# The five GpSimd sums of a pair for the second MLP product, put one at a time over the steps of the next pair

## The chip, the cores and the metric

The kernel runs on one NeuronCore of a Trainium2 chip. The engines have short names in the profile: PE is TensorE (matmuls), PEld its weight loads, DVE is VectorE, ACT is ScalarE, POOL is GpSimd, SP is the sync engine, whose queue issues the DMAs. Each engine works through its own queue in order, and waits for the others through semaphores. The metric is the device time of one execution in microseconds (us). Before the change it is 2529.06 us, the median of three runs (2527.83 to 2530.4).

## What is computed

Two layers of a decoder on 1024 tokens of width 1024. Each layer is an attention (the first a sparse one with compressed, selected and windowed keys, the second a sliding window with sinks) and an MLP, with norms and a conditioning vector `c` around both:

```python
def squared_relu_mlp(h, w_up, w_down):
    a = jax.nn.relu(h @ w_up)
    return (a * a) @ w_down

def reference(x, c, positions, ada_w, ada_b, norm_g, ...):
    cond = jax.nn.silu(c)
    for i in range(DEPTH):                       # 2
        mod = cond @ ada_w[i] + ada_b[i]
        sh1, sc1, g1, sh2, sc2, g2 = jnp.split(mod, 6, axis=-1)
        h = modulate(rms_norm(x, norm_g[i, 0]), sh1, sc1)
        ...                                      # attention gives y
        x = x + (1 + g1)[:, None, :] * rms_norm(y, norm_g[i, 1])
        h = modulate(rms_norm(x, norm_g[i, 2]), sh2, sc2)
        y = squared_relu_mlp(h, mlp_w_up[i], mlp_w_down[i])
        x = x + (1 + g2)[:, None, :] * rms_norm(y, norm_g[i, 3])
    return x
```

The change touches the MLP alone: `w_up` is 1024 x 4096, `w_down` is 4096 x 1024, all in f32.

## The kernel before

**Products.** Both MLP products are done with seven block products in place of eight, in the manner of Strassen and Winograd: sums and differences of blocks are formed first. Each f32 factor is split in a high part (a copy in a shorter format, `hi`) and the rest (`lo`), and three matmuls, hi times hi, lo times hi and hi times lo, stand for one (`mm3`, L572 to L574). A product of the first stage is twelve matmuls of 128x512.

**The up stage** (`mlp_up`) walks over 16 pairs `q` of column blocks of `w_up`. A pair needs seven products, in the order p = 1, 2, 6, 5, 7, 3, 4. For the first six pairs (`PAIRS0`) the products 1 and 2 are made ahead of all others, a stretch that the code calls the ramp. For each product a step of `prep` makes the weights, `AHEAD` products ahead:

```python
            elif p == 6:
                t(new(1), w[21], w[22], op=ALU.add)          # L1325, DVE
                t(new(2), sums[1], w[11], op=ALU.subtract)   # L1326, DVE
...
            elif p == 7:
                nc.gpsimd.tensor_tensor(r, w.pop(11), w.pop(21), op=ALU.subtract)   # L1332, POOL
...
            nc.scalar.activation(hi, r, AF.Copy)                                    # L1342, ACT
            nc.vector.tensor_tensor(lo, r, hi.bitcast(F32), op=ALU.subtract)        # L1343, DVE
```

L1336 is the like of L1332 for p = 3. So the weights of a product go DMA (`w`, L547), a sum on DVE or POOL (`ws`), the copy on ACT (`wt`), the rest on DVE (the same `wt`), PE. After a product, `evac` adds the PSUM bank `b` into the pair's tiles `u` (DVE, L1373), and ACT applies Relu (L1385) and Square (L1386), or copies (L1375).

**The five sums.** When a pair's last product is done, its four blocks of hidden values lie in two tiles `a` and `b` (both `u` in the trace). The second MLP product needs five sums or differences of these, which `combine` makes on POOL: four into two tiles `sx` (L1418), one into `sy` (L1429). SP writes them and two blocks of `u` to DRAM (`s`, L1422 to L1430), from where the down stage reads them. `combine` returns a list of stages; `chain` runs one stage and puts the next behind the following step.

**The order.** The Python steps are not the order on the engines. A scheduler takes the program order as priority, works out when operands will be ready, and lays out every engine's queue; then tiles get their buffers. Forty slots of 128x1024 f32 serve `sx`, `u`, `wt`, most raw weights `w`, and the tiles of the down stage together; a tile that takes a slot waits for the last reader of the one that had it. Conditioning weights (`adaw`, L311, multiplied on DVE by L321 and L323 into `ada`) are loaded and used in the gaps of the up stage. The first halves of `w` of later pairs and the `adaw` tiles share a ring of three buffers.

**The down stage** (`mlp_down`) then loads `w_down` (`wr`), sums it on POOL (L1476, L1477), splits it (`st`, ACT L1491 and DVE L1492) and multiplies.

Of the kernel before, what the change touches and what calls it, by code (L numbers as in the profile page):

```python
# [82 lines left out]
def spread(a, b):  # L83

    out, n = [], 0
    for k, f in enumerate(b):
        while n < len(a) and n * len(b) <= k * len(a):
            out.append(a[n])
            n += 1
        out.append(f)  # L90
    return out + a[n:]


class Trunk:
# [1271 lines left out]
    def mlp_up(self, up, side, sd, begin):  # L1366
        nc = self.nc
        R, order, before, left, _ = up
        U, banks, last = {}, {}, len(order) - 1

        def evac(q, p, o):
            a, b = U[q][0], U[q][-1]
            act, add = nc.scalar.activation, lambda out, y: nc.vector.tensor_tensor(out, o, y, op=ALU.add)  # L1373
            if p == 1:
                act(a[:, 1], o, AF.Copy)  # L1375
            elif p == 6:
                add(b[:, 0], a[:, 1])
            elif p == 5:
                add(a[:, 1], b[:, 0])
            else:  # L1380
                v, y = {2: (a[:, 0], a[:, 1]), 7: (b[:, 1], a[:, 1]), 3: (a[:, 1], a[:, 1]), 4: (b[:, 0], b[:, 0])}[p]
                add(v, y)
                if p == 7:
                    add(b[:, 0], b[:, 0])
                act(v, v, AF.Relu)  # L1385
                act(v, v, AF.Square)  # L1386

        def product(i):
            q, p = order[i]

            def part(j):
                if j == 0:
                    if p == 1:
                        U[q] = [self.slot("u", F32, [P, 2, 512])]
                    elif p == 6:
                        U[q].append(self.slot("u", F32, [P, 2, 512]))
                    banks[i] = self.bank()
                hi, lo = R[p][j]
                for z in range(2):
                    k = 2 * j + z  # L1400
                    s = tuple(left[i][:, y, k * P:(k + 1) * P] for y in range(2))
                    self.mm3(banks[i], s, (hi[:, z], lo[:, z]), k == 0, k == 3)
                if q == len(sd) - 1:
                    R[p][j] = None
                if j == 1:
                    left.pop(i)
                    evac(q, p, banks.pop(i))
            return [lambda j=j: part(j) for j in range(2)]

        def combine(q):  # L1410
            a, b = U.pop(q)
            d, z = sd[q], {}

            def two(n, *ops):
                def f():
                    z[n] = self.slot("sx", F32, [P, 2, 512])
                    for k, (x, y, op) in enumerate(ops):
                        nc.gpsimd.tensor_tensor(z[n][:, k], x, y, op=op)  # L1418
                return f

            def put():
                nc.sync.dma_start(d[:, 0], b[:, 1])  # L1422
                nc.sync.dma_start(d[:, 5], a[:, 0])
                nc.sync.dma_start(d[:, 1:3], z[0])

            def put2():
                nc.sync.dma_start(d[:, 3:5], z[1])
                v = self.t2("sy")
                nc.gpsimd.tensor_tensor(v, a[:, 1], b[:, 1], op=ALU.add)  # L1429
                nc.sync.dma_start(d[:, 6], v)  # L1430

            A, B = ALU.add, ALU.subtract
            return [two(0, (a[:, 0], b[:, 1], A), (b[:, 0], b[:, 1], B)), put,
                    two(1, (a[:, 0], b[:, 0], A), (a[:, 1], a[:, 0], B)), put2]

        ramp, steps = [], []
        for i, (q, p) in enumerate(order):
            own = spread(before(i), product(i))
            if p == 4:
                own.append(lambda q=q: self.later(lambda: self.chain(combine(q)), 1))  # L1440
            (ramp if i < 2 * PAIRS0 + 10 else steps).extend(own)
        self.go(ramp)
        self.go(spread(side, steps[:-LEAD_DOWN]) + spread(begin, steps[-LEAD_DOWN:]))
# [405 lines left out]
```

## Time and profile before

| | us |
|---|---|
| median of three runs | 2529.06 |
| lowest and highest | 2527.83, 2530.4 |
| the profiled execution | 2529.18 |
| its span in the trace | 2527.4 |
| PE busy in it | 2390.7 |
| DVE busy | 1924.7 |
| ACT busy | 1403.4 |
| POOL busy | 1323.6 |

The up stage of the first layer (layer 0) lies at about 950 to 1230 us of the trace and that of the second (layer 1) at about 1940 to 2220 us. Matmuls are pipelined: a matmul row shows 0.39 us, but in an unbroken stretch the next one starts about 0.22 us later. In the timelines, a number in brackets is how long the engine was idle ahead of the instruction, with what ended the wait.

### The profile page before, as it was taken

What the parts mean: (1) busy time and instruction counts of PE and PEld (TensorE: products, weight loads), DVE (VectorE), ACT (ScalarE), POOL (GpSimd) and SP (SyncE); (2) the same over time, 40 slices, a digit from 0 to 9 for tenths busy, and PEclk for the clock granted to TensorE, in tenths of its full rate; (3) what the DMA queues carried; (4) which work ended last, traced back from release to release, by engine and by line L of the source; (5) the groups of instructions that cost most, each with busy time, mean ns of one, the idle gap of its engine ahead of it and who ended that gap; (6) DMA issues with size and microseconds to landing.
All of it is one profiled execution on the core that took longest, in us unless ns stands there. A gap on an engine that the chain in (4) does not pass through costs nothing.

```text
span 2527.4 us, 36711 instructions
## 1 busy us (share of the span) xinstructions
PE 2390.7 (95%) x11974; PEld 1988.7 (79%) x11974; DVE 1924.7 (76%) x3723; ACT 1403.4 (56%) x2959; POOL 1323.6 (52%) x1308
## 2 busy tenths in 40 slices
PE   6889999999999988999899999988999999999997
PEld 4779888888887767777788887867877688888886
DVE  7865579999895487777799768676768766687756
ACT  4532368898983473454435445377876354545433
POOL 4320566565662146555764622577744554694533
PEclk8999999999999999999999999999999999999999
DMA  7367723132226536556888654444323555597654
GB/s 281 100 216 238 249 80 97 39 93 62 78 68 150 141 117 200 188 199 201 316 327 321 239 186 173 142 140 111 84 86 120 183 176 183 193 319 243 224 186 171
DMA packets 239287, 437.14 MB, mean 173 GB/s; under 512 B 19236, under 2 KB 122872, under 8 KB 239096
## 3 DMA queue, kind: packets, MB, share of 16 engines
q1 hardware_dynamic: 210296, 405.44, 47.6%
q0 software_dynamic: 28800, 29.36, 4.9%
q8 instruction: 94, 1.54, 0.3%
q14 instruction: 97, 0.79, 0.1%
HBM read 320.42 MB, written 114.31 MB: 172 GB/s over the span
## 4 chain that ended last, share of the span: by engine, by line
PE 38%; DVE 5%; POOL 4%; issue 3%; DMA 3%; ACT 2%; SPq 0%; POOLq 0%; DVEq 0%; ACTq 0%
PE b L574 12%; PE b L572 12%; PE b L573 12%; POOL sx L1418 1%; DVE ada L323 1%; POOL qv L637 1%; ACT p L888 1%; PE o L925 1%; PE b L880 1%; DMA wr<-in_mlp_w_down_dram 1%; PE b L903 1%; DMA w<-in_mlp_w_up_dram 1%; DVE hl L1254 1%; DVE wt L1343 1%; DMA adaw<-in_ada_w_dram 0%
## 5 line engine op out<-in xcount | busy, mean ns | idle before, releaser
L572 PE MATMUL b<-hh,wt 128*128 128x512 f32 x896 | 355.5, 397 | 15.5 <-ACT wt L1342 15.3
L574 PE MATMUL b<-hh,wt 128*128 128x512 f32 x896 | 350.7, 395 | 8.7 <-DVE wt L1343 8.5
L573 PE MATMUL b<-st,st 128*128 128x512 f32 x896 | 349.8, 391 | 4.6 <-DVE st L1492 4.6
L573 PE MATMUL b<-hl,wt 128*128 128x512 f32 x896 | 352.2, 393 | 0.0
L574 PE MATMUL b<-st,st 128*128 128x512 f32 x896 | 348.9, 390 | 0.0
L572 PE MATMUL b<-st,st 128*128 128x512 f32 x896 | 330.8, 390 | 2.7 <-DVE u L1373 1.6
L888 ACT ACTIVATE p<-p,nm 128x256 f32<-128x256 f32 (+7 forms) x384 | 250.4, 656 | 46.9 <-DVE nm L884 45.5
L1031 POOL TENSOR_SCALAR p<-p,rl,nsam 128x640 f32<-128x640 f32 (+7 forms) x256 | 199.7, 793 | 136.3 <-DVE rl L1029 98.9
L1492 DVE TENSOR_TENSOR st<-wr,st 128x1024 fp32r<-128x1024 f32 (+1 forms) x128 | 189.8, 1482 | 55.8 <-ACT st L1491 36.5
L910 DVE TENSOR_TENSOR pT<-b,pT 128x512 fp32r<-128x512 f32 (+1 forms) x334 | 215.3, 657 | 21.7 <-ACT pT L909 21.3
L1491 ACT ACTIVATE st<-wr 128x1024 fp32r<-128x1024 f32 (+1 forms) x128 | 122.6, 958 | 195.1 <-POOL wr L1477 89.9
L1492 DVE TENSOR_TENSOR st<-sr,st 128x1024 fp32r<-128x1024 f32 (+1 forms) x128 | 200.8, 1569 | 32.6 <-ACT st L1491 30.4
L572 PEld LDWEIGHTS b<-hh,wt 128*128 128x128 f32 x896 | 170.7, 191 | 58.5 <-ACT wt L1342 24.6
L574 PEld LDWEIGHTS b<-hh,wt 128*128 128x128 f32 x896 | 170.2, 190 | 50.7 <-DVE wt L1343 15.2
L909 ACT ACTIVATE pT<-b 128x512 fp32r<-128x512 f32 (+1 forms) x334 | 185.5, 577 | 42.7 <-PE b L903 40.5
L925 PE MATMUL o<-pT,kv 128*128 128x512 f32 x484 | 194.7, 442 | 7.1 <-DVE pT L910 7.0
L573 PEld LDWEIGHTS b<-st,st 128*128 128x128 f32 x896 | 168.6, 188 | 41.5 <-DVE st L1492 6.8
L903 PE MATMUL b<-ident,p 128*128 128x128 f32 x1296 | 195.4, 274 | 4.7 <-POOL p L1629 2.5
L572 PEld LDWEIGHTS b<-st,st 128*128 128x128 f32 x896 | 168.5, 188 | 39.0 <-DVE u L1373 2.4
L1343 DVE TENSOR_TENSOR wt<-ws,wt 128x512 fp32r<-128x512 f32 x128 | 139.4, 1100 | 77.6 <-ACT wt L1342 76.8
L573 PEld LDWEIGHTS b<-hl,wt 128*128 128x128 f32 x896 | 170.4, 190 | 34.9
L574 PEld LDWEIGHTS b<-st,st 128*128 128x128 f32 x896 | 168.6, 188 | 34.7
(277 smaller groups left out, 6039.6 us busy)
## 6 DMA issues: line engine op xcount, KB each, us to landing
adaw<-in_ada_w_dram SPq DMA_DIRECT2D x96, 512.0 KB, 4.8
sr<-s SPq DMA_DIRECT2D x96, 512.0 KB, 4.5
wr<-in_mlp_w_down_dram SPq DMA_DIRECT2D x96, 512.0 KB, 6.6
w<-in_mlp_w_up_dram SPq DMA_DIRECT2D x76, 512.0 KB, 4.7
s<-sx SPq DMA_DIRECT2D x64, 512.0 KB, 4.2
x<-x SPq DMA_DIRECT2D x48, 512.0 KB, 3.2
s<-u SPq DMA_DIRECT2D x64, 256.0 KB, 2.2
we<-in_mlp_w_down_dram SPq DMA_DIRECT2D x64, 256.0 KB, 4.4
```

Source lines behind the costliest of these rows:

```text
L572: mm(out, s[0], m[0], start=first, stop=False)
L573: mm(out, s[0], m[1], start=False, stop=False)
L574: mm(out, s[1], m[0], start=False, stop=last)
L888: self.nc.scalar.activation(p, p, AF.Exp, scale=-1.0, bias=nm, accum_out=l)
L903: nc.tensor.transpose(pt[:, g * P:(g + 1) * P], p[:, cols], self.ident)
L909: nc.scalar.activation(x[:, 0, 0:w], pt[:, 0:w], AF.Copy)
L910: nc.vector.tensor_tensor(x[:, 1, 0:w], pt[:, 0:w], x[:, 0, 0:w].bitcast(F32), op=ALU.subtract)
L925: nc.tensor.matmul(out, s, m[:, z], start=n == 0 and z == 0, stop=n == len(tiles) - 1 and z == 1)
L1031: nc.gpsimd.tensor_scalar(ps[g], ps[g], rl[:, g:g + 1], gate[:, g, b:b + 1], op0=ALU.mult, op1=ALU.mult)
L1343: nc.vector.tensor_tensor(lo, r, hi.bitcast(F32), op=ALU.subtract)
L1491: nc.scalar.activation(hi, r, AF.Copy)
L1492: nc.vector.tensor_tensor(lo, r, hi.bitcast(F32), op=ALU.subtract)
```

## The change

The two stages that made two sums each become four stages that make one each, with empty stages (`none`) between, and the sum `sy` with its write becomes a stage of its own, after the second write. The chain has nine stages where it had four, two of them empty. The same instructions are issued, with the same operands; from L1435 on, a line's number is one higher.

```diff
--- before.py
+++ after.py
@@ -1411,12 +1411,10 @@
             a, b = U.pop(q)
             d, z = sd[q], {}
 
-            def two(n, *ops):
-                def f():
+            def one(n, k, x, y, op):
+                if k == 0:
                     z[n] = self.slot("sx", F32, [P, 2, 512])
-                    for k, (x, y, op) in enumerate(ops):
-                        nc.gpsimd.tensor_tensor(z[n][:, k], x, y, op=op)
-                return f
+                nc.gpsimd.tensor_tensor(z[n][:, k], x, y, op=op)
 
             def put():
                 nc.sync.dma_start(d[:, 0], b[:, 1])
@@ -1425,13 +1423,16 @@
 
             def put2():
                 nc.sync.dma_start(d[:, 3:5], z[1])
+
+            def last():
                 v = self.t2("sy")
                 nc.gpsimd.tensor_tensor(v, a[:, 1], b[:, 1], op=ALU.add)
                 nc.sync.dma_start(d[:, 6], v)
 
             A, B = ALU.add, ALU.subtract
-            return [two(0, (a[:, 0], b[:, 1], A), (b[:, 0], b[:, 1], B)), put,
-                    two(1, (a[:, 0], b[:, 0], A), (a[:, 1], a[:, 0], B)), put2]
+            none = lambda: None
+            return [lambda: one(0, 0, a[:, 0], b[:, 1], A), none, lambda: one(0, 1, b[:, 0], b[:, 1], B), put,
+                    lambda: one(1, 0, a[:, 0], b[:, 0], A), none, lambda: one(1, 1, a[:, 1], a[:, 0], B), put2, last]
 
         ramp, steps = [], []
         for i, (q, p) in enumerate(order):
```

The scheduler turns this into another order on all engines, in the up stages above all. On POOL, in a pair of the middle of layer 0 (its five sums go to `sx` and `sy`; the number after a name tells one tile from another). Before:

```order
L1418 TENSOR_TENSOR sx_12680<-u_12507,u_12577 128x512
L1418 TENSOR_TENSOR sx_12697<-u_12507 128x512
L1429 TENSOR_TENSOR sy_12708<-u_12507,u_12577 128x512
L1332 TENSOR_TENSOR ws_12711<-w_12585 128x512
L1336 TENSOR_TENSOR ws_12734<-w_12587,ws_12658 128x512
L1418 TENSOR_TENSOR sx_12680<-u_12577 128x512
L1418 TENSOR_TENSOR sx_12697<-u_12507,u_12577 128x512
```

After:

```order
L1332 TENSOR_TENSOR ws_12704<-w_12582 128x512
L1336 TENSOR_TENSOR ws_12731<-w_12584,ws_12658 128x512
L1417 TENSOR_TENSOR sx_12680<-u_12507,u_12573 128x512
L1429 TENSOR_TENSOR sy_12736<-u_12507,u_12573 128x512
L1417 TENSOR_TENSOR sx_12709<-u_12507 128x512
L1417 TENSOR_TENSOR sx_12680<-u_12573 128x512
L1417 TENSOR_TENSOR sx_12709<-u_12507,u_12573 128x512
```

The two sums of weights (`ws`) have moved from the middle of the five sums to ahead of all of them, and the five stand in one unbroken row.

On DVE, in the ramp of layer 0, from the first add into the second tile of the second pair, `u_11082` before and `u_11078` after (L1373 are adds of products, L1343 rests of weights, L1325 and L1326 sums of weights). Before:

```order
L1373 TENSOR_TENSOR u_11082<-b_11083,u_10688 128x512
L1373 TENSOR_TENSOR u_10688<-b_11111,u_11082 128x512
L1373 TENSOR_TENSOR u_11082<-b_11132,u_10688 128x512
L1373 TENSOR_TENSOR u_11082<-b_11132,u_11082 128x512
L1343 TENSOR_TENSOR wt_11108<-w_10981,wt_11108 128x512
L1325 TENSOR_TENSOR ws_11125<-w_11093,w_11095 128x512
L1373 TENSOR_TENSOR u_10688<-b_11152,u_10688 128x512
L1326 TENSOR_TENSOR ws_11127<-ws_11125,w_11093 128x512
L1343 TENSOR_TENSOR wt_11129<-ws_11127,wt_11129 128x512
L1373 TENSOR_TENSOR u_11082<-b_11173,u_11082 128x512
L1343 TENSOR_TENSOR wt_11149<-ws_11125,wt_11149 128x512
```

After:

```order
L1373 TENSOR_TENSOR u_11078<-b_11079,u_10688 128x512
L1373 TENSOR_TENSOR u_10688<-b_11106,u_11078 128x512
L1325 TENSOR_TENSOR ws_11122<-w_11087,w_11089 128x512
L1373 TENSOR_TENSOR u_11078<-b_11132,u_10688 128x512
L1373 TENSOR_TENSOR u_11078<-b_11132,u_11078 128x512
L1326 TENSOR_TENSOR ws_11124<-ws_11122,w_11087 128x512
L1373 TENSOR_TENSOR u_10688<-b_11152,u_10688 128x512
L1343 TENSOR_TENSOR wt_11103<-w_10981,wt_11103 128x512
L1343 TENSOR_TENSOR wt_11126<-ws_11124,wt_11126 128x512
L1343 TENSOR_TENSOR wt_11149<-ws_11122,wt_11149 128x512
L1343 TENSOR_TENSOR wt_11170<-ws_11168,wt_11170 128x512
```

The sum of L1325, which waits for a load of weights, stood behind the rest of `w_10981` and behind four adds; now it stands ahead of that rest and behind two adds.

On SP, in the same ramp, with the engines and DMA queues for which each issue waits (`L547` are loads of weights, `L1424` and `L1427` of before are `L1422` and `L1425` of after, writes of sums). Before:

```order
L1430 DMA s_1_10637<-sy_11214 128x512 [waits DMAHW4_49,Pool_49]
L1424 DMA s_1_10637<-sx_11189 128x1024 [waits DMAHW5_49,Pool_49]
L547 DMA w_11219<-in_mlp_w_up_dram 128x4x256 [waits DMAHW2_49,DMAHW6_49,Activation_49,Pool_49]
L1427 DMA s_1_10637<-sx_11202 128x1024 [waits Pool_49]
L547 DMA w_11340<-in_mlp_w_up_dram 128x4x256 [waits DMAHW0_49,DVE_49]
L311 DMA adaw_11368<-in_ada_w_dram 128x1024 [waits DMAHW3_49,DMAHW1_49,DVE_49]
L311 DMA adaw_11446<-in_ada_w_dram 128x1024 [waits DVE_49,Pool_49]
```

After:

```order
L311 DMA adaw_11281<-in_ada_w_dram 128x1024 [waits DMAHW3_49,DVE_49,Pool_49]
L1430 DMA s_1_10637<-sy_11237 128x512 [waits DMAHW4_49,Pool_49]
L547 DMA w_11212<-in_mlp_w_up_dram 128x4x256 [waits DMASW1_49,DMAHW5_49,DVE_49,PE_49]
L1422 DMA s_1_10637<-sx_11189 128x1024 [waits DMAHW6_49,Pool_49]
L1425 DMA s_1_10637<-sx_11214 128x1024 [waits DMAHW7_49,Pool_49]
L547 DMA w_11333<-in_mlp_w_up_dram 128x4x256 [waits DMAHW0_49,DVE_49]
L311 DMA adaw_11368<-in_ada_w_dram 128x1024 [waits DMAHW1_49,Pool_49]
```

The load that was `w_11219` is `w_11212` now: it waited for ACT and POOL, takes another buffer now and waits for DVE and PE, and stands ahead of both writes of the sums of that pair.

On DVE, in the middle of layer 0, around the rest of the weights `ws_12711` of before, `ws_12704` of after (L323 multiplies a loaded `adaw`). Before:

```order
L323 SCALAR_TENSOR_TENSOR ada_12596<-adaw_12796,cond,ada_12596 128x1024
L1343 TENSOR_TENSOR wt_12683<-ws_12656,wt_12683 128x512
L1373 TENSOR_TENSOR u_12577<-b_12663,u_12577 128x512
L323 SCALAR_TENSOR_TENSOR ada_12596<-adaw_12884,cond,ada_12596 128x1024
L1343 TENSOR_TENSOR wt_12713<-ws_12711,wt_12713 128x512
L1373 TENSOR_TENSOR u_12689<-b_12718,u_12689 128x512
L1343 TENSOR_TENSOR wt_12736<-ws_12734,wt_12736 128x512
L1373 TENSOR_TENSOR u_12739<-b_12740,u_12689 128x512
L323 SCALAR_TENSOR_TENSOR ada_12596<-adaw_12957,cond,ada_12596 128x1024
```

After:

```order
L323 SCALAR_TENSOR_TENSOR ada_12596<-adaw_12796,cond,ada_12596 128x1024
L1373 TENSOR_TENSOR u_12507<-b_12640,u_12507 128x512
L323 SCALAR_TENSOR_TENSOR ada_12596<-adaw_12879,cond,ada_12596 128x1024
L1343 TENSOR_TENSOR wt_12682<-ws_12656,wt_12682 128x512
L1373 TENSOR_TENSOR u_12573<-b_12663,u_12573 128x512
L323 SCALAR_TENSOR_TENSOR ada_12596<-adaw_12957,cond,ada_12596 128x1024
L1343 TENSOR_TENSOR wt_12706<-ws_12704,wt_12706 128x512
L1343 TENSOR_TENSOR wt_12733<-ws_12731,wt_12733 128x512
L1373 TENSOR_TENSOR u_12685<-b_12713,u_12685 128x512
```

Of the three multiplications by L323 shown, two stood ahead of that rest; now all three do, and the middle one has also passed the rest before it, `wt_12683`, which is `wt_12682` now.

## Rows read from the trace of the kernel before

**Rows 1.** First part of the page: engine, busy us, share of span, instructions.
```profile
PE 2390.7 (95%) x11974; PEld 1988.7 (79%) x11974; DVE 1924.7 (76%) x3723; ACT 1403.4 (56%) x2959; POOL 1323.6 (52%) x1308
```

**Rows 2.** Busy time by stretch: length, then busy us and instructions of each engine.
```profile
core 0: us, PE busy (x) PEld busy (x) DVE busy (x) ACT busy (x) POOL busy (x), PEclk, DMA share, GB/s
...
1228.00:1260.00 32.00, 25.59 (x99) 18.90 (x98) 29.13 (x19) 13.20 (x17) 31.87 (x16) 0.95 0.95 353
...
2020.00:2220.00 200.00, 200.00 (x891) 165.23 (x890) 135.82 (x174) 104.12 (x169) 116.64 (x82) 1.00 0.54 191
...
1161.50:1165.50 4.00, 3.93 (x10) 3.16 (x11) 2.67 (x5) 2.30 (x4) 0.00 (x0) 0.57 0.94 290
```

**Rows 3.** Timeline of PE, middle of layer 0: start, duration, line, tiles, [idle before].
```profile
1158.08 0.50 PE L572 MATMUL b<-hh,wt 128*128 128x512 f32 x1 [0.33 <-ACT wt L1342]
...
1161.57 0.78 PE L574 MATMUL b<-hh,wt 128*128 128x512 f32 x1 [2.76 <-DVE wt L1343]
...
1165.32 0.39 PE L574 MATMUL b<-hh,wt 128*128 128x512 f32 x1
```

**Rows 4.** Timeline of PE in the ramps of layer 0 and layer 1.
```profile
963.64 0.80 PE L572 MATMUL b<-hh,wt 128*128 128x512 f32 x1 [2.41 <-ACT wt L1342]
...
979.86 0.50 PE L572 MATMUL b<-hh,wt 128*128 128x512 f32 x1 [0.70 <-ACT wt L1342]
...
984.55 0.79 PE L574 MATMUL b<-hh,wt 128*128 128x512 f32 x1 [2.92 <-DVE wt L1343]
...
1986.66 0.50 PE L572 MATMUL b<-hh,wt 128*128 128x512 f32 x1 [2.77 <-ACT wt L1342]
```

**Rows 5.** Timeline of POOL, the pair of the middle of layer 0.
```profile
1149.44 1.30 POOL L1418 TENSOR_TENSOR sx<-u,u 128x512 f32<-128x512 f32 x1 [9.21 <-ACT u L1386]
...
1154.50 1.76 POOL L1332 TENSOR_TENSOR ws<-w 128x512 f32<-128x512 f32 x1
...
1158.72 2.25 POOL L1418 TENSOR_TENSOR sx<-u,u 128x512 f32<-128x512 f32 x1
```

**Rows 6.** Timeline of DVE, from three places.
```profile
957.88 0.68 DVE L1343 TENSOR_TENSOR wt<-w,wt 128x512 fp32r<-128x512 f32 x1
960.97 0.69 DVE L1325 TENSOR_TENSOR ws<-w,w 128x512 f32<-128x512 f32 x1 [2.41 <-DMA w<-in_mlp_w_up_dram]
...
1157.57 2.28 DVE L323 SCALAR_TENSOR_TENSOR ada<-adaw,cond,ada 128x1024 f32<-128x1024 f32 x1 [1.88 <-DMA adaw<-in_ada_w_dram]
1159.77 1.74 DVE L1343 TENSOR_TENSOR wt<-ws,wt 128x512 fp32r<-128x512 f32 x1
...
1162.04 0.68 DVE L1343 TENSOR_TENSOR wt<-ws,wt 128x512 fp32r<-128x512 f32 x1
...
1984.52 0.69 DVE L1325 TENSOR_TENSOR ws<-w,w 128x512 f32<-128x512 f32 x1 [2.06 <-DMA w<-in_mlp_w_up_dram]
```

**Rows 7.** DMA issues of SP (no duration of the transfer), from three places.
```profile
956.51 0.38 SPq L547 DMA_DIRECT2D w<-in_mlp_w_up_dram  x1
...
1147.46 0.33 SPq L311 DMA_DIRECT2D adaw<-in_ada_w_dram  x1
...
1153.41 0.33 SPq L311 DMA_DIRECT2D adaw<-in_ada_w_dram  x1
...
1978.23 0.38 SPq L547 DMA_DIRECT2D w<-in_mlp_w_up_dram  x1
```

**Rows 8.** Timeline of ACT, ramp of layer 0.
```profile
962.30 0.63 ACT L1385 ACTIVATE u<-u 128x512 f32<-128x512 f32 x1 [3.55 <-DVE u L1373]
```

**Rows 9.** What ended DVE's idle time before L1325, whole run: us, times.
```profile
  DMA w<-in_mlp_w_up_dram: 27.8, 16
```

**Rows 10.** Timelines of PE and POOL where the down stage begins in layer 0.
```profile
1252.06 0.49 PE L572 MATMUL b<-st,st 128*128 128x512 f32 x1 [1.19 <-ACT st L1491]
1253.33 0.50 PE L573 MATMUL b<-st,st 128*128 128x512 f32 x1 [0.77 <-DVE st L1492]
```
```profile
1246.41 2.27 POOL L1476 TENSOR_TENSOR wr<-wr,we 128x512 f32<-128x512 f32 x1
```

## The prediction

> **What bounds the kernel now.** The first part of the page shows PE busy for 2390.7 of 2527.4 us [rows 1], so only time in which PE stands still, or runs slowly, can be won. The busy time by stretch says where: in 2020 to 2220 us, the later part of the up stage of layer 1, PE is busy for 200 of 200 us [rows 2]. It starts a matmul every 200 / 891 = 0.224 us there. Nothing that POOL does in that stretch can make it shorter. The losses lie in four other places. The timeline of PE shows them as idle times, each with the instruction that ended it: the ramp of layer 0 (2.41, 0.70 and 2.92 us) and of layer 1 (2.77) [rows 4], one point in the middle of layer 0 (0.33 and 2.76) [rows 3], and the beginning of the down stage in layer 0 (the last two are 1.19 and 0.77) [rows 10]. All are waits for weights: ACT's copy or DVE's rest.
>
> Such a wait costs more than its idle time. After the one that ends at 1161.57, nine steps take until 1165.32, which is 3.75 us where 9 x 0.224 = 2.02 would do [rows 3]. The granted clock of 1161.5 to 1165.5 is 0.57, most of it at the lower level, 1.2 GHz, where 2020 to 2220 shows 1.00, 2.4 GHz [rows 2]. So a wait of this size costs its length and about 1.7 us more.
>
> POOL, whose sums are moved, is not the bound: its timeline shows it idle for 9.21 us, waiting for the hidden values, before a pair's first sum [rows 5]. But it makes two sums of weights per pair, and its `sx` tiles hold slots that weight loads wait for. Through these two the change can reach PE.
>
> **What the change removes and adds.** No instruction is added or removed; the empty stages issue nothing. Sums, writes and what the scheduler puts around them move. The order of POOL shows that the five sums are not spread there: the weight sums now stand first, and the five follow in a row. So what I cost is this new order, place by place.
>
> *Middle of layer 0.* Before, POOL waited 9.21 us for a square, made three sums from 1149.44 on, and only then the weight sum of 1154.50, which ended at 1156.26 [rows 5]. ACT's copy of it came late: PE's 0.33 us. DVE then took a multiplication of conditioning weights, waiting 1.88 us for its load, until 1159.85, and PE's weights were ready at 1161.51 [rows 6]: PE's 2.76 us. With the slow steps this point costs 0.33 + 2.76 + 1.7 = 4.8 us. After, the weight sums are made in POOL's idle time and the 0.33 us goes. What DVE does ahead is late next: two multiplications stand ahead of the rest that PE needs, and their loads follow one another. A load took 4.16 us (issued at 1153.41, waited for until 1157.57) [rows 6, 7]. The second of three loads can be issued right after the first, at about 1147.5 [rows 7], instead of 1153.41, since the buffer that it takes is free one multiplication earlier; so it lands at about 1151.7. Its multiplication takes 1.2 to 2.3 us and ends at 1153 to 1154; the third load waits for that, lands at about 1157.5, and is multiplied until 1158.7 to 1159.8. The rest takes 0.68 to 1.74 us (the two durations in [rows 6]), so it ends between 1159.4 and 1161.5, against 1161.51. I take 1160.7, because both multiplications can meet POOL's sums: a gain of 0.33 + 0.8, and 0.9 for slow steps that fall away half of the time, together **2 us**, with bounds of -0.5 (a later load) and 4.8.
>
> Here a page matters. The two durations, 1.74 us while POOL works and 0.68 us at 1162.04 when POOL is idle, are of one shape [rows 5, 6]. The Trainium skill, page "SBUF — State Buffer", section "Who interferes with whom", says that a DVE instruction with two SBUF inputs contends with a GpSimd instruction that reads SBUF. The trace agrees, with these two numbers. By that rule alone, taking the sums out of the way of the rests would bring 1.06 us wherever a rest ends a wait of PE, and pushing the five sums into one row against them would take as much; the sum above would move by that and no further.
>
> *Ramp of layer 0.* Two points. The first is the wait that ends at 963.64. It comes from a load of weights, issued at 956.51 and waited for by L1325 until 960.97, so 4.4 us [rows 6, 7]. After, its buffer comes free one product earlier, so it may be issued about 3.4 us (a product is 12 x 0.224 = 2.7 us) sooner and land at about 957.5. But L1325 now stands ahead of two adds and of the rest of `w_10981`, which DVE could begin at 957.88 before [rows 6]. From 957.5: L1325 and two adds at 0.7 each (L1325's duration [rows 6]; an add has the same shape), then ACT's Relu, Square and copy at 0.63 each [rows 8], make 961.5, where PE wants the copy at 963.64 - 2.41 - 2.7 = 958.5. So the wait moves five microseconds ahead and is 3.0 for 2.41 us long, which is -0.6 in a chain of estimates; I count 0, with bounds of -2 (the load takes the 6.3 us seen in layer 1) and 4.1 (it is gone, with its slow steps). The second point, 0.70 + 2.92 + 1.7 = 5.3 us [rows 4], comes from the next weight sums, which stood behind the next load and a multiplication. After, that load waits for PE and not for the sums in `sx`, and the weight sums come ahead of the multiplication, so these weights are ready several microseconds ahead. I take 5.3 less 1.3 us, half of the first point's wait, for the next such load, since there too L1325 has moved ahead of the adds: **4 us** for the ramp, bounds -2 and 9.4.
>
> *Ramp of layer 1.* The same, with less luck. The load issued at 1978.23 was waited for until 1984.52, so 6.3 us [rows 6, 7], and PE lost 2.77 and 1.7 us at 1986.66 [rows 4]. After, it waits for PE and may go at about 1974.5, landing at 1980.8. L1325 stands ahead of an add and of the rest that PE wants at about 1980.6; with L1325, the add and L1326 at 0.6 to 0.7 each, and the rest, that is ready at 1983.3. PE waits some 2.7 us there and no more at 1986.66. I take **1 us**, bounds -1.5 and 4.5.
>
> *Into the down stage, layer 0.* POOL is busy for 31.87 of 32 us in 1228 to 1260 [rows 2]. The pair of `w_down` sums that began at 1246.41 [rows 10] moves ahead of the last two of the five sums, so up to 4.5 us earlier, but what it passes must still be done. The two waits at its end are 1.19 + 0.77 us, with 1.7 for slow steps: **1 us**, bounds 0 and 3.7. The remaining stretch of layer 1 is full on PE and counts nothing; small exchanges in the second attention count 0, within 1 us either way, since they move no wait that I found.
>
> The sum is 2 + 4 + 1 + 1 = 8 us. The profiled execution took 2529.18 us, 0.1 over the median, so **2521 us**.
>
> **The rivals.** *Given back.* The waits only change places: the second point of layer 0's ramp goes, but a later L1325 takes it back, and the middle stays as it is, because its three loads follow one another anyhow. For it: the up stage ends with PE full, and each of the four terms has a new wait behind the removed one. Against: two waits of PE (0.70, 2.92) have no successor in the new order that I can see. It gives about 2 us of gain, 2527. *Slower.* DVE's queue is in order, and L1325 waits for a load. Before, it waited 27.8 us in 16 times in the whole run [rows 9], mostly with adds behind it that PE did not need at once. In the new order the rest of a product that PE is about to want stands behind it. If half of that time reaches PE, 13.9 us are lost, and against the 8 us that makes 2529.2 + 13.9 - 8 = 2535. It decides where a load lands later than about 2.7 us (L1325, two adds, the rest) before PE wants that rest. Against it: the same loads are issued 3 to 4 us sooner. *That it does nothing,* since POOL makes the sums in a row anyhow, is the first rival's time.
>
> **How the numbers follow.** The forecast, 0.54: 2521, and by itself 2513 to 2524. Given back, 0.28: 2524 to 2533. Slower, 0.18: 2534 to 2540. About 0.2% or 5 us is what a measurement of this kernel can tell from no change, so faster 0.54, same 0.28, slower 0.18. All four terms at their best make 22 us, 2507, which needs everything to go well; the range begins at 2510 and ends at 2535, in the middle of the slower case.
>
> **What would show it.** Right: in the ramp of layer 0 no wait of PE above 1 us between 970 and 990; at 1158 to 1162 one wait below 2.5 us; on POOL the two weight sums inside what was the idle time of 9 us; and loads of `w` issued 3 us sooner. Wrong: waits of PE for DVE's rest, with L1325 waiting for its load just before on DVE, at places where there were none, and low clock behind them; or a wait at 1161 as long as it was, behind a multiplication that waits for its load.

## The result: slower, and where the profile after shows it

The changed kernel takes 2544.5 us (median of four runs, 2543.37 to 2547.3), the kernel before 2528.44 us (four runs). The ratio is 1.0067, with a 95% interval of 1.0054 to 1.0079: about 16 us slower, where 2521 had been forecast, and outside the range that ended at 2535. The profiled execution has a span of 2543.0 us.

The first lines of the page after, to be read beside [rows 1]:

```profile
span 2543.0 us, 36723 instructions
...
PE 2396.3 (94%) x11974; PEld 1991.6 (78%) x11974; DVE 1944.2 (76%) x3723; ACT 1400.0 (55%) x2959; POOL 1332.7 (52%) x1308
```

The same 11974 matmuls. The span grew by 15.6 us, PE's busy time by 5.6 and its idle time by the other 10. About 3 of the 5.6 us are slow steps: 18 more than before that take some 0.4 us where 0.22 is usual (an estimate, counted from the starts of the matmuls).

The timeline of PE after, where it stood still in the up stages: first two points in the ramp of layer 0 (to be read beside [rows 4]), then later pairs of layer 0, the middle ([rows 3] before), and the ramp of layer 1.

```profile
963.74 0.80 PE L572 MATMUL b<-hh,wt 128*128 128x512 f32 x1 [4.23 <-ACT wt L1342]
...
999.60 0.50 PE L572 MATMUL b<-hh,wt 128*128 128x512 f32 x1 [3.05 <-ACT wt L1342]
...
1051.60 0.50 PE L574 MATMUL b<-hh,wt 128*128 128x512 f32 x1 [1.55 <-DVE wt L1343]
...
1087.20 0.50 PE L574 MATMUL b<-hh,wt 128*128 128x512 f32 x1 [0.66 <-DVE wt L1343]
1091.15 0.50 PE L574 MATMUL b<-hh,wt 128*128 128x512 f32 x1 [0.93 <-DVE wt L1343]
...
1116.74 0.50 PE L574 MATMUL b<-hh,wt 128*128 128x512 f32 x1 [2.22 <-DVE wt L1343]
...
1174.70 0.50 PE L574 MATMUL b<-hh,wt 128*128 128x512 f32 x1 [3.97 <-DVE wt L1343]
...
1996.77 0.79 PE L574 MATMUL b<-hh,wt 128*128 128x512 f32 x1 [4.43 <-DVE wt L1343]
```

The waits between 1050 and 1120 us have no counterpart in before. All but two of these waits end with DVE's rest of a split (L1343).

The table of waits of DVE and PE names what DVE did ahead of those rests: for 1020 to 1240 us, first before, then after (us in total, times, longest).

```profile
DVE ws L1325 <- DMA w<-in_mlp_w_up_dram: 8.6, 5, 2.5
...
PE b L574 <- DVE wt L1343: 2.9, 2, 2.8
```
```profile
DVE ws L1325 <- DMA w<-in_mlp_w_up_dram: 12.2, 5, 3.2
PE b L574 <- DVE wt L1343: 9.8, 7, 4.0
...
DVE ws L1325 <- issue: 2.7, 1, 2.7
```

And for 2030 to 2240 us, the later pairs of layer 1, before and after:

```profile
DVE ws L1325 <- DMA w<-in_mlp_w_up_dram: 9.4, 6, 3.3
```
```profile
DVE ws L1325 <- DMA w<-in_mlp_w_up_dram: 19.2, 7, 3.2
```

L1325 waits longer for its load, and PE's waits for rests rise from 2.9 to 9.8 us in the first of the two stretches (in each, one long wait, 2.76 and 3.97 us, is that of the middle). In the second stretch PE did not stand still at all before. After, it does for 3.1 us, and only 0.9 of these are waits for rests of weights; the others are for other work in DVE's queue:

```profile
PE b L574 <- DVE wt L1343: 0.9, 2, 0.6
PE b L436 <- DVE adag L432: 0.8, 1, 0.8
PE b L572 <- DVE u L1373: 0.8, 1, 0.8
PE b L573 <- DVE st L1493: 0.6, 2, 0.4
```

Here `adag` belongs to the conditioning weights, `u` is an add, and `st` a rest of the down stage. So some 10 us more of waiting at L1325 go with 3 us of idle time of PE there, and with slower steps around each wait.

One such place in layer 0 as DVE sees it. The timeline of DVE after, with the copies that ACT makes there, and then DVE at the same products in before:

```profile
1110.35 0.68 DVE L1373 TENSOR_TENSOR u<-b,u 128x512 f32<-128x512 f32 x1
1114.19 0.69 DVE L1325 TENSOR_TENSOR ws<-w,w 128x512 f32<-128x512 f32 x1 [3.17 <-DMA w<-in_mlp_w_up_dram]
1114.80 0.68 DVE L1373 TENSOR_TENSOR u<-b,u 128x512 f32<-128x512 f32 x1
1115.40 0.68 DVE L1326 TENSOR_TENSOR ws<-ws,w 128x512 f32<-128x512 f32 x1
1116.00 2.97 DVE L1343 TENSOR_TENSOR wt<-w,wt 128x512 fp32r<-128x512 f32 x3
```
```profile
1112.26 1.14 ACT L1342 ACTIVATE wt<-w 128x512 fp32r<-128x512 f32 x2
1114.25 0.63 ACT L1342 ACTIVATE wt<-w 128x512 fp32r<-128x512 f32 x1 [0.86 <-DMA w<-in_mlp_w_up_dram]
```
```profile
1103.20 0.68 DVE L1373 TENSOR_TENSOR u<-b,u 128x512 f32<-128x512 f32 x1
1103.80 0.68 DVE L1325 TENSOR_TENSOR ws<-w,w 128x512 f32<-128x512 f32 x1
1104.40 1.28 DVE L1343 TENSOR_TENSOR wt<-w,wt 128x512 fp32r<-128x512 f32 x2
1105.60 0.68 DVE L1326 TENSOR_TENSOR ws<-ws,w 128x512 f32<-128x512 f32 x1
```

After, DVE is free at 1111.0 and stands for 3.17 us at L1325, whose data isn't there. Behind it stand three rests. Two of them need nothing of that load: ACT had made their copies by 1112.9 and 1113.4. Only the third copy, like L1325, waits for a load that lands at 1114.2. The first rest begins at 1116.00 and PE waits until 1116.74. Before, L1325 did not wait here, and two rests came right behind it, ahead of L1326.

The issues of SP after at this place show why the load was late:

```profile
1104.73 0.39 SPq L1430 DMA_DIRECT2D s<-sy  x1
1108.21 0.33 SPq L1422 DMA_DIRECT2D s<-sx  x1
1109.90 0.38 SPq L547 DMA_DIRECT2D w<-in_mlp_w_up_dram  x1
```

The load is issued at 1109.90 and lands 4.3 us later. Two waits for POOL hold it up. It stands in SP's queue behind a write of sums, which went out at 1108.21, as soon as POOL had finished them; and then it waits 1.3 us itself, until POOL has finished its next sum for `sx`. Before, the load went out at 1097.99, which in the time of after is about 1106.4 (the kernel had lost 8.4 us by then). This is not one place alone. SP's waits from 900 to 2300 us in which a load (L547) was released by one of POOL's sums, before and then after:

```profile
SPq L547 <- POOL sx L1418: 4.5, 4, 1.2
```
```profile
SPq L547 <- POOL sx L1417: 15.9, 13, 1.3
```

Where the 16 us went can be read from the starts of the same matmul in both traces. The table gives how much each kernel lost (+) or won (-) in each stage against the one profiled run of before, in us; the times are those of before. All kernels of the experiments below are in it. The fourth column, in which little differs between them, shows how far such numbers can be trusted: it is -1 to -4 us for nearly all of them, so it is the run of before that was slow there. Moving a boundary by some 5 us changes single numbers by up to 1.6 us. The stretch ahead of 935 us is left out: there the traces differ from that of before by -1.7 to +7.7 us, in no order that follows the changes, so a row does not add up to the difference of two times.

| kernel | 935-1020, ramp of layer 0 | 1020-1140, later pairs | 1140-1300, last pairs and into the down stage | 1300-1945 | 1945-2030, ramp of layer 1 | 2030-2205, later pairs | 2205-2300 |
|---|---|---|---|---|---|---|---|
| after | 3.2 | 8.3 | 1.5 | -4.2 | 0.1 | 3.2 | 2.5 |
| e1, layer 0 only | 3.1 | 7.8 | 1.4 | -3.5 | 0.6 | 0 | 0 |
| e2, layer 1 only | 0.4 | 0.3 | -1.0 | -2.1 | -2.9 | 6.7 | 2.4 |
| e3, after, L1325 late | 6.6 | 0.8 | -6.4 | -3.5 | -4.6 | 0 | 0 |
| e4, before, L1325 late | 3.1 | -2.6 | -2.6 | -3.8 | -1.9 | 0 | 0 |
| e5, sy one step later | 1.6 | 1.5 | 0.6 | -1.9 | 0.3 | 6.2 | 1.1 |
| e6, copies without order | 2.6 | 8.2 | 1.7 | 0.8 | 0.3 | 4.3 | 2.4 |
| e7, late in the ramps | 5.1 | 7.8 | 0.9 | -1.3 | -4.0 | 4.6 | 2.5 |
| e8, single sums, sy fourth | 2.2 | 0.3 | 1.0 | -1.9 | -2.8 | 0 | 0 |
| e9, pairs, nine stages | 2.2 | 7.2 | 1.0 | -2.5 | -1.1 | 3.4 | 1.7 |
| e10, late in later pairs | 3.5 | 2.4 | -6.8 | -4.1 | -0.8 | 0 | 0 |
| e11, new chain, best | -2.5 | 2.1 | -6.0 | -2.9 | -4.6 | 0 | 0 |
| e12, old chain, best | -0.3 | -0.8 | -0.7 | -1.8 | -1.8 | 0 | 0 |

In after's row the two columns of later pairs and the last one hold 14 of 15 us. Just there the prediction had counted nothing.

### The profile page after: what moved, and what is told of

It reads as the page before. It is cut to its first block, busy times and chain, and to the rows that moved or that the text cites. A ratio compares the mean times of both kernels' runs of the same rounds, so it can differ in the third digit from the quotient of the medians.

```text
span 2543.0 us, 36723 instructions
## 1 busy us (share of the span) xinstructions
PE 2396.3 (94%) x11974; PEld 1991.6 (78%) x11974; DVE 1944.2 (76%) x3723; ACT 1400.0 (55%) x2959; POOL 1332.7 (52%) x1308
## 5 line engine op out<-in xcount | busy, mean ns | idle before, releaser
L1385 ACT ACTIVATE u<-u 128x512 f32<-128x512 f32 x128 | 80.7, 631 | 219.3 <-DVE u L1373 219.1
```

## The experiments

The theory was that DVE stands at L1325 for a load of weights, ahead of rests that PE needs. The rivals are these: the unbroken row of five sums on POOL collides with DVE's two-input instructions; the sums' slots hold up the loads; single sums are dearer than pairs.

**One layer at a time.** A counter in `mlp_up` chooses the chain (this cut and those of the other chains below are shortened):

```diff
+            if old:                      # layer 1 in e1, layer 0 in e2
+                return [both of z[0], put, both of z[1], put2 and last]
             return [lambda: one(0, 0, ...), none, ..., put2, last]
```

> The new chain of nine stages in layer 0 alone; layer 1 keeps the four stages of before. The trace of after lies 11 to 12 us behind that of before at the end of layer 0's MLP and 15.6 at the end. If the loss is made on the spot in each up stage (theory: DVE's queue waits for a load of weights, in L1325, ahead of rests that PE needs): 2539 to 2541. If the two layers act on each other, or the loss is one of layer 1 (rival): below 2535.

> The new chain in layer 1 alone; layer 0 as before. Theory, loss on the spot: 2532 to 2534, the 4 to 5 us that the trace of after loses between 1990 us and the end. With the run of layer 0 alone it should add up to the 16 us of the whole change. Rival, the layers act on each other: no sum.

Measured against 2526.68 us of before, which ran again beside the new kernels: 2538.41 (ratio 1.0044, 1.0030 to 1.0059) and 2531.40 (1.0015, 1.0001 to 1.0028). The excesses, 11.7 and 4.7 us, add up to 16.4, where the whole change costs 16.1. So each layer's loss is made on the spot, as expected; both times lie about half a us below the ranges forecast for them, which had been reckoned from a slightly slower before.

**L1325 held back.** In `prep`, for p = 6:

```diff
-                t(new(1), w[21], w[22], op=ALU.add)
+                n1 = new(1)
+                for h in (1, 3, 2):
+                    if i - h in left and order[i - h][1] in (4, 1):
+                        nc.vector.tensor_copy(n1[:, 0, 0:1], left[i - h][:, 1, 0:1].bitcast(F32))
+                        break
+                t(n1, w[21], w[22], op=ALU.add)
```

> The changed kernel, with one thing more: L1325 of a pair may not begin before the rest (L1343) of the last product of the pair before. A one-column copy from that rest into L1325's own output, which L1325 then overwrites, makes it wait; 31 such copies are added on DVE. POOL's order, the five sums in a row, and the nine stages stay. Theory, the loss is DVE's queue standing at L1325 behind a load: 2526 to 2532, and PE's waits at 963 and 1996 us of after are gone. Rival, POOL's unbroken sums collide with DVE's two-input instructions, or the slots that the sums now take hold up the loads: 2540 to 2547, as after. A third case, the copies cost by themselves: at most 31 x 0.1 us = 3 us more.

> The kernel before with the same one-column copies that keep L1325 behind the rest of the last product of the pair before. In before L1325 stood ahead of that rest in some pairs too, and waited 27.8 us in 16 times for its load. Theory: 2522 to 2528, a gain of up to 6 us, more than the 31 copies of 0.1 us cost. Rival, L1325's place did not matter in before since only adds stood behind it: 2528 to 2532.

e3: 2525.63 us (0.9994, 0.9981 to 1.0007). It is as fast as before. The timeline of DVE of e3, where L1325 waited 3.17 us in after; L1325 is L1330 there, L1343 is L1348, L1328 the copy:

```profile
1111.96 1.29 DVE L1348 TENSOR_TENSOR wt<-w,wt 128x512 fp32r<-128x512 f32 x2 [1.29 <-ACT wt L1347]
1113.17 0.15 DVE L1328 COPY ws<-wt 128x1 f32<-128x1 f32 x1
1113.59 0.69 DVE L1348 TENSOR_TENSOR wt<-w,wt 128x512 fp32r<-128x512 f32 x1 [0.27 <-ACT wt L1347]
1114.20 0.69 DVE L1330 TENSOR_TENSOR ws<-w,w 128x512 f32<-128x512 f32 x1
```

Its SP issues the load at the same point of its queue, again behind a write of sums and a wait for POOL:

```profile
1107.26 0.33 SPq L1427 DMA_DIRECT2D s<-sx  x1
1108.95 0.38 SPq L547 DMA_DIRECT2D w<-in_mlp_w_up_dram  x1
```

The sum begins when it began in after, 1114.20 for 1114.19. The load lands at 1112.85, and reckoned against the same matmuls that is within half a us of after's. But the rests are done ahead of the sum, from 1111.96 on, where they began at 1116.00 in after; PE does not wait. Nor does the sum wait for its load in any stretch of e3. Over the whole run its loads still wait for POOL's sums, 13.4 us in 12 times, nearly as in after, and its five sums stand in a row. So neither the row nor the late loads cost the time by themselves: it takes L1325 ahead of the rests. Not all that was expected held: PE's waits in the ramp of layer 0 did not go, they changed cause (6.6 us lost there, with DVE waiting 9.6 us for loads of conditioning weights), while the last pairs and the ramp of layer 1 gained.

e4: 2525.62 us (0.9993, 0.9980 to 1.0006). A gain of 1.1 us, not told apart from none. In before itself L1325's place cost little.

Not all that e3 takes back was lost by the change. The wait in the middle of layer 0, which stood in before too, is short with L1325 held back, whichever chain runs: none of PE's waits there is above 0.5 us in e3, e4 and e10, and 1140 to 1170 us gain 4.1 to 4.2 us in each. What the change itself lost, and e3 does not, are the later pairs: 0.8 for 8.3 us in layer 0, and nothing in layer 1.

**Is it the copies?**

```diff
+                n1 = new(1)
+                nc.vector.tensor_copy(n1[:, 0, 0:1], self.ones)
+                t(n1, w[21], w[22], op=ALU.add)
```

> The changed kernel with the same 31 one-column copies into L1325's output, but taken from a constant, so that they do not hold L1325 back. L1325 keeps its place of after. Theory, only the place matters: 2542 to 2549, as after or up to 31 x 0.15 = 4.7 us above. Rival, the copies help by themselves (another layout of buffers, another schedule): 2526 to 2535.

2549.94 us against 2528.12 (1.0082, 1.0061 to 1.0102). The interval overlaps that of after (1.0054 to 1.0079), so a cost of the copies is not shown; but they do not help. The order that they force is what helps in e3.

**Ramps or later pairs?** The same hold, with `and q <= PAIRS0` in e7 and `and q > PAIRS0` in e10:

> The changed kernel with L1325 held behind the rest of the last product of the pair before in the first seven pairs of each layer only (the ramps and one pair more). Theory: the trace of after has lost about 5 us at 1020 us, the end of layer 0's ramp, and nothing by the end of layer 1's, so the ramps give back about 5 us of 16: 2537 to 2541. If the ramps alone make the loss, as the prediction's third case has it: 2526 to 2531. If the loss lies in the later pairs alone: 2543 to 2546.

> The changed kernel with L1325 held behind the last rest of the pair before in the later pairs alone (from the eighth on), the complement of the run with the ramps. By stages, after lost 8.3 us between 1020 and 1140 us and 5.6 between 2030 and 2250 us. Theory: these go, 2527 to 2533, and the run of the ramps (no gain) and this one (all of it) add up to the run with both. Rival, some other part of the new order in those pairs costs: 2538 or more.

e7: 2545.36 us (1.0066, 1.0051 to 1.0081), as after. The case called theory, 2537 to 2541, was a miss, and that of a loss in the later pairs alone came true: the hold costs 2 us more in the ramp of layer 0 and gains 4 in that of layer 1, and the later pairs lose all that they lost in after. e10: 2525.61 us against 2528.20 (0.9994, 0.9986 to 1.0003): as fast as before, with 2.4 us lost for 8.3 in the later pairs of layer 0, nothing in those of layer 1, and the gain in the middle. So the loss lay in the later pairs. Their tables of waits for 1020 to 1240 us say the same; e7 first, then e10 (in e10 no wait of the sum for its load is left):

```profile
DVE ws L1330 <- DMA w<-in_mlp_w_up_dram: 12.9, 5, 3.6
PE b L574 <- DVE wt L1348: 10.5, 7, 4.0
```
```profile
PE b L574 <- DVE wt L1348: 0.6, 3, 0.2
```

**Which part of the edit moves L1325?** Three chains, none of which touches L1325 itself:

```diff
 e5 (before, sy a stage of its own)
-   [two(0, ...), put, two(1, ...), put2 with sy]
+   [two(0, ...), put, two(1, ...), put2, last]
 e8 (after, sy in the fourth stage)
-   [one, none, one, put, one, none, one, put2, last]
+   [one, none, one, put with last, one, none, one, put2]
 e9 (before, sums in pairs, nine stages)
-   [two(0, ...), put, two(1, ...), put2 with sy]
+   [two(0, ...), none, none, put, two(1, ...), none, none, put2 with sy, none]
```

> The kernel before with one line of the change alone: the sum sy and its write become a stage of their own, the fifth, one step later than before. The other four sums stay in pairs, and no empty stage is added. In the order that comes of this, L1325 stands ahead of the last rest of the pair before in nearly all pairs of both layers, by as many places as in the changed kernel. Theory, the place of L1325 is what costs: 2541 to 2546, as after. Rival, the spreading of the sums over nine steps costs, one at a time: 2528 to 2532.

> The changed kernel, sums one at a time over eight stages with two empty ones, but sy made in the fourth stage together with the first writes, as early as it stood in the chain of before. In its order L1325 stands four to seven places ahead of the last rest in the ramps, as in after, but within one place of it in most later pairs. Theory, the place costs: the loss of the ramps stays, that of the later pairs goes, 2531 to 2539. Rival, single sums spread over the steps cost: 2543 to 2546, as after.

> The sums in pairs as before, but the chain stretched to nine stages with empty ones, the last two sums in the fifth and sy in the eighth. In its order L1325 stands three to seven places ahead of the last rest of the pair before in 13 of 15 pairs of layer 0 and in all of layer 1, nearly as in after. Theory, the lateness of the chain moves L1325 and its place costs: 2539 to 2546. Rival, making the sums one at a time is what costs: 2527 to 2532.

e9: 2540.21 us (1.0052, 1.0039 to 1.0065): pairs of sums on nine stages lose nearly as much as single ones, in the same later pairs. e8: 2528.42 us (1.0007, 0.9994 to 1.0019): single sums over eight stages, with `sy` early, lose nothing there. Its waits in 1020 to 1240 us:

```profile
DVE ws L1325 <- DMA w<-in_mlp_w_up_dram: 3.6, 6, 1.1
PE b L574 <- DVE wt L1343: 3.2, 2, 2.7
```

So making the sums one at a time is not what costs. e8 differs from after in the place of `sy` alone, and that is enough to undo the loss; its last two sums are as late as in after. Two things are gone with it: no load in e8 is released by a sum for `sx` (in e9 12 are, in after 13), and in the later pairs L1325 stands ahead of the last rest mostly by one place, where it is mostly by three to five in after and e9. How often it stands ahead is not the sign: 11 and 12 of 15 pairs in the two layers of e8, more than in before. e8 came out below what was expected of it, 2531 to 2539: in its ramps L1325 stands as far ahead as in after, but the ramp of layer 1 gained 2.8 us.

e5: 2537.45 us (1.0034, 1.0021 to 1.0047). Here the expectation told the order wrongly. In the kernel that ran, L1325 stands ahead of the last rest in 6 of 15 pairs of layer 0 and 5 of 15 of layer 1, fewer than in before (8 and 11). It lost all the same, 6.2 of its 9 us in the later pairs of layer 1, where L1325 waits 11.1 us in 6 times, not much more than the 9.4 of before. Its loads are released by POOL's sums as in before, 4.5 us in 4 times. So L1325 does not explain this run. PE's longest wait in those pairs, 1.88 us, is for `adag`, and DVE waits 6.3 us there for conditioning weights where before had 3.2; whether that is the cause is not settled.

**A version that beats both.** By the table, the new chain with L1325 held back wins in the last pairs of layer 0 and in the ramp of layer 1, and loses in the ramp of layer 0. e11 takes the old chain for the six pairs of that ramp, the new one elsewhere, and holds L1325 back except in that ramp; e12 is the kernel before with the same hold:

```diff
+            if lay == 0 and q < PAIRS0:            # e11 only
+                return [both of z[0], put, both of z[1], put2 and last]
...
+                    if i - h in left and order[i - h][1] in (4, 1) and (lay == 1 or q > PAIRS0):
```

> An attempt at a version that beats both: the old chain in the ramp of layer 0, the new chain elsewhere, and L1325 held behind the last rest except in that ramp. By stages of the runs so far, each against before: ramp of layer 0 about 0, later pairs 1, into the down stage -6, ramp of layer 1 -4, its later pairs 0: 2517 to 2523, if stages add up. If what a stage gives depends on what came before it: 2524 to 2529.

> The kernel before with L1325 held behind the last rest except in the ramp of layer 0. By stages of the run with that hold everywhere: later pairs of layer 0 -2.6, into the down stage -2.6, ramp of layer 1 -1.9, and the 3.1 us that its ramp of layer 0 lost are left out: 2519 to 2523 if stages add up, else 2524 to 2528.

e11: 2520.29 us against 2528.20 (0.9966, 0.9953 to 0.9979), the only one whose whole interval lies more than 0.2% below before. That is in the range for stages that add up. e12: 2523.46 us (0.9987, 0.9977 to 0.9996), between its two ranges: its later pairs and the way into the down stage gave 1.5 us in place of 5.2. e11's first lines, and DVE's and PE's rows of its table of waits for 1945 to 2030 us, where before lost 2.77 us and more [rows 4]; L1349 is ACT's copy, L1350 the rest:

```profile
span 2522.4 us, 36747 instructions
...
PE 2389.5 (95%) x11974; PEld 1987.7 (79%) x11974; DVE 1938.3 (77%) x3748; ACT 1398.5 (55%) x2959; POOL 1333.4 (53%) x1308
```
```profile
PE b L573 <- ACT wt L1349: 1.8, 4, 0.7
PE b L575 <- DVE wt L1350: 0.9, 2, 0.6
```

## Why the prediction was wrong, step by step

**What fell.** The result is nearest to the prediction's third case, "slower", which had 0.18, 2535 and at most 2540: DVE's in-order queue waiting at L1325 with a rest behind it. As a rival the mechanism was named rightly; the forecast left it out, and the steps below put it in the wrong place and made it too small.

- *"The remaining stretch of layer 1 is full on PE and counts nothing."* This is the step that failed. That PE is busy 200 of 200 us [rows 2] says that it has no wait to lose, so nothing can be won there. It does not say how far a wait is off. DVE's L1325 already waited 9.4 us there in before, in 6 times, and PE stood still for none of it. After, it waited 19.2 us, and PE stood still for 3.1. The later pairs of both layers cost 8.3 us in layer 0 (1020 to 1140) and 3.2 + 2.5 in layer 1, 14 us in all. The prediction looked for the price at the four places where PE already waited. In the orders the table of places was there to be read: over all pairs, L1325 stands ahead of the last rest of the pair before in 13 of 15 pairs of layer 0 and in 15 of 15 of layer 1 after, against 8 and 11 before. (By e8 the count alone is not enough: the distance and the lateness of the load count too.)
- *"If half of that time reaches PE, 13.9 us are lost", less a gain of 8.* The loss of 13.9 is near to the 14 measured, but by luck: it is half of the 27.8 us that L1325 waited in before [rows 9], and after it waited 56.4 us in 21 times. The waits themselves doubled, which the prediction did not reckon with. And the gain of 8 did not come.
- *"The same loads are issued 3 to 4 us sooner."* Nearly true of the loads in the ramps that were looked at: against the same matmuls they went 2.5 us sooner in layer 0 and 3.2 us in layer 1. In the later pair shown above the load waits behind a write of sums and for a sum itself, and went out at 1109.90 where before's, moved by the loss up to there, would have gone at 1106.4.

**The terms.**

- *Ramp of layer 0, 4 us won.* It lost 3.2. The second point went, as forecast: no wait above 1 us is left between 970 and 990. The first was priced at 3.0 us and took 4.23 [rows 4 has 2.41], with 14 slow steps behind it where before had 8. Two terms of its chain were too small. The load went out at 955.07, which is 954.0 in the time of before, not 953.1; and L1325 took 1.67 us beside POOL's sums, not 0.7. A third point came up at 999.60, 3.05 us, the same wait at the next load, for which 1.3 us had been set aside.
- *Middle of layer 0, 2 us won.* It lost 0.7. The last of the chained loads was sized at 4.16 us and took 4.8, so DVE stood 3.61 us ahead of its multiplication, and PE 3.97 us [rows 3 have 0.33 and 2.76]. The rows of that place:

```profile
1166.43 0.33 SPq L311 DMA_DIRECT2D adaw<-in_ada_w_dram  x1
```
```profile
1171.22 1.76 DVE L323 SCALAR_TENSOR_TENSOR ada<-adaw,cond,ada 128x1024 f32<-128x1024 f32 x1 [3.61 <-DMA adaw<-in_ada_w_dram]
1172.90 2.35 DVE L1343 TENSOR_TENSOR wt<-ws,wt 128x512 fp32r<-128x512 f32 x2
```

- *Ramp of layer 1, 1 us won.* It came out even (0.1). The forecast that the wait moves one product ahead, to the rest, was right; it was 4.43 us for 2.7, in part since the load took 7 us (1987.21 to 1994.22) for 6.3. By the prediction's own price, 1.7 us on top of a wait, a new wait of 2.7 us in place of 2.77 would have left no gain; the 1 us was too much by its own sum.
- *Into the down stage, 1 us won.* 1.5 lost from 1140 to 1300, of which 0.7 is the middle's. With L1325 held back in the later pairs, the same new chain wins 6 to 7 us in this stretch (e3, e10, e11). But over 4 of these lie in the middle, between 1140 and 1170, where the old chain with L1325 held back wins as much (4.2 in e4, 3.7 in e12). What is left for the way into the down stage is 1.2 to 2.4 us, about the size of the forecast; that the new order of the sums makes it is not shown by itself.

**What held.** The five sums do stand in a row on POOL; that did no harm: e3 keeps this row and has none of the loss. DVE instructions beside POOL's sums did take longer at single places (the 1.67 us of L1325 above), but that is not what made the kernel slower: the median of the rests of `ws` is 0.88 us after, for 1.10 before, and 1.18 in e3, which is as fast as before. The rule of the Trainium skill, page "SBUF — State Buffer", section "Who interferes with whom", that a DVE instruction with two SBUF inputs contends with a GpSimd instruction that reads SBUF, agrees with the single places and decided nothing here. That a wait brings slow steps behind it was seen again: at 1116.74 the steps that follow are 0.43 us apart for 3 us.

**What stays open.** Why the scheduler places L1325 earlier when `sy` is late (after, e8 and e9 show that it does, not by which of its reckonings); what e5 loses; and how the 3 us of PE's idle time in the later pairs of layer 1 divide among L1325's waits and other work of DVE, of which only the sum is shown by e3 and e10, where they are gone.

## What to carry to other kernels

An engine that is full has no time to win but may have time to lose: ask for each engine that feeds it which instruction in its queue waits for a DMA, and what then stands behind it. Where a scheduler lays out the queues, compare the place of such instructions over the whole run, not only where the profile shows waits today. Here a one-column copy of 0.15 us each, which ties the sum that waits for a load to the last urgent work, brought the changed kernel back to the time of before.

## What was not expected of the chip

A load of 512 KB for L1325 took from 4.3 us (1109.90 to 1114.19) to 7.0 us (1987.21 to 1994.22) from its issue to the instruction that waited for it, in one execution. And a chain of stages on POOL that is longer, with not one instruction more, can cost 12 us (e9) or nothing (e8), by the place of one sum in it.
